# Two blocks' rows turned by VectorE and DMA moves instead of TensorE in a float32 decoder layer

## The chip, the cores and the metric

The kernel runs on one core of one Trainium2 chip. The metric is the device time of one execution in microseconds (us), the median of several runs. A profile of one execution gives the busy time of each engine: TensorE (PE, and PEld for its weight loads), VectorE (DVE), ScalarE (ACT), GpSimd (POOL), and SyncE (SP), which issues nearly all DMA transfers.

## The reference

One decoder layer over 2048 tokens of 1024 channels in float32: a normalised input goes through one combined projection into two mixers (a gated short convolution and a gated linear recurrence), their outputs through W_out back into x, then a multilayer perceptron (MLP) with a squared relu, then a last norm.

```python
    x = x + jnp.einsum('bsc,cd->bsd', y, w_out[l])
    h = rmsnorm(x, norm_mlp_g[l])
    z = jnp.square(jax.nn.relu(jnp.einsum('bsd,df->bsf', h, w_mlp_in[l])))
    x = x + jnp.einsum('bsf,fd->bsd', z, w_mlp_out[l])
```

The change concerns the second of these lines: the norm of x, with its weight, and the transposition of its rows that the third line needs.

## The kernel before

Tokens are worked in blocks of 512, two blocks (b and b+1) at a time, so the program goes through the same stages twice, for a first and a second pair. Every matrix product of two blocks is done with seven products instead of eight (a Strassen-Winograd scheme). The products are numbered 1 to 7 and run in the order 1, 2, 6, 5, 7, 3, 4 in the MLP (`ORDER`, L40). Each operand is split into a high and a low part of a shorter float format, `hi` by a copy on ScalarE and `lo` by a subtraction on VectorE (`split_into`, L196 to L198), and each product takes three matmuls (high by high, high by low, low by high).

Three stages matter here.

The out-projection (`pair_before_mlp`, L2135). Class `WOut` multiplies the mixers' outputs by W_out, product by product. A product has four tiles of 128 tokens with 18 matmuls each; after each tile VectorE adds the PSUM result into the residual `x` (`add`, L2112 to L2116). The products run in the order 1, 2, 6, 5, 3, 7, 4. The functions `in_sixth`, `in_fifth`, `in_third`, `in_seventh` and `in_fourth` are called after each tile of the product they are named for, and hold what the other engines do beside it. After product 3 block b's rows of x are complete; after product 4 block b+1's.

The norm and the turn. For each tile, ScalarE sums the squares (`square`, L2349), VectorE and ScalarE make the factor (`root`, L2360), and the scaled rows go to a tile `xs`: one half by VectorE, one by ScalarE (`scaled`, L2373, L2380 and L2381). The MLP needs the rows turned, with channels on partitions. Block b is turned in 32x32 blocks by VectorE (`cut_squares`, L2390) and then by DMA moves that bring every 32 partitions onto 128 (`move_squares`, L2400 to L2405); the norm weight is multiplied in after that (`gain_rows`, L2424). Block b+1 is turned by TensorE: `turn` (L1980) makes eight transposes of 128x128 into PSUM, and ScalarE copies each out, multiplying in the norm weight (L1991). Two of a pair's four turns stand inside product 4 of the out-projection and just behind it, two after the first and second MLP product (`turns`, L2478, called from `mlp`).

The MLP's first half (`mlp`, L2509, class `Up`, L605). Hidden columns come in eight groups of 512. The sequence starts with products 1 and 2 of groups 0, 1 and 2, which need block b alone, and goes on with their products 6, 5, 7, 3, 4, which need sums and differences of both blocks' turned rows (`rest`, L2482, `fifth`, L2496, `later_operands`, L2033). `Up.prepare` splits a weight tile two products ahead, `Up.sums` makes the weight sums, `Up.drain` (L671) takes results out of PSUM, applies the squared relu and spills to DRAM. The PSUM buffers are four of 2 x 512 columns. In the opening, three stay with product 1 of the three groups, and the fourth passes from one group's product 2 to the next.

What sets the order. Within the out-projection the order of TensorE, ScalarE and VectorE is that of the program text (`by_hand`, L2645). From the MLP on only TensorE's order is stated so; the order on ScalarE, VectorE and SP comes from the framework's list scheduler, by priority and by free buffers. SP is scheduled throughout. A DMA instruction on SP waits in order: what stands behind one that waits, waits too.

Of the kernel before, what the change touches and what calls it, by code (L numbers as in the profile page):

```python
# [9 lines left out]
F32 = mybir.dt.float32  # L10
# [38 lines left out]
T_ROOM = 15  # L49
LEADS = (0, 0, 2, 3, 2, 1, 2, 2, 2, 2, 2, 3, 2, 2)  # L50
# [41 lines left out]
def block_kernel(  # L92
# [11 lines left out]
    mlp_g_t,  # L104
# [12 lines left out]
    cp.tile([P, 120], F32, name="pad")  # L117
    hp = ctx.enter_context(tc.tile_pool(name="hp", bufs=2))
# [315 lines left out]
    def new_h():  # L434
        return (
            hp.tile([P, KD, TB], F32R, tag="h", name="h_hi"),
            hp.tile([P, KD, TB], F32R, tag="h", name="h_lo"),
        )
# [166 lines left out]
    class Up:  # L605
# [33 lines left out]

        def prepare(self, i):  # L640
            src = {1: "a11", 2: "a12", 6: "s2", 5: "a21", 7: "s3", 3: "a12", 4: "a22"}[i]
            self.ready[i] = split_new(getattr(self, src), wtile, "w")
# [27 lines left out]

        def drain(self, i, Z):  # L671
            def snap(ps):
                t = temp("snap")
                made_at["snap"] = nc.scalar.copy(t, ps).ins  # L674
                return t

            def square(t):
                if self.s < 3 or self.by_act:
                    nc.scalar.activation(t, t, AF.Relu)  # L679
                    nc.scalar.activation(t, t, AF.Square)  # L680
                else:
                    V.scalar_tensor_tensor(t, t, 0.0, t, MAX, MUL)
# [9 lines left out]
            elif i == 2:  # L692
                for j in range(2):
                    c = by_token(self.c11, j)
                    V.tensor_add(c, by_square(self.y, j), c)
                square(self.c11)
                keep(1, self.c11)
# [4 lines left out]
            elif i == 7:  # L702
                V.tensor_add(self.c22, self.x, self.c22)  # L703
                square(self.c22)
                keep(4, self.c22)
            elif i == 3:
                V.tensor_add(self.c12, self.w, self.c12)
                square(self.c12)
# [1271 lines left out]
    def turn(xs, t, r, g=None):  # L1980

        ps = psum("tps", (P, KD, P))
        for k in range(KD):
            nc.tensor.transpose(ps[:, k, :], xs[:, k // 4, k % 4 * P : (k % 4 + 1) * P], ident)
        sl = slice(t * P, (t + 1) * P)
        if g is None:
            for q in range(4):
                nc.scalar.copy(r[q][:, :, sl], ps[:, 2 * q : 2 * q + 2, :])
# [713 lines left out]
```

## Time and profile before

| | us |
|---|---|
| median of 3 runs | 2084.69 (2084.52 to 2084.88) |
| the profiled execution, its own time | 2084.75 |
| its span in the profile | 2082.9 |
| busy: PE, DVE, ACT, POOL | 2072.8, 1635.8, 1140.9, 46.4 |

The span is the time from the first to the last instruction; the execution's own time holds another 1.85 us around it. Rows of the instruction views begin with the start in us from the beginning of the span and the duration in us; "x4" behind a row is a count of merged instructions. "Matmul busy" is counted with the pipelined ends of matmuls, so the time between one start and the next is the better measure of what a matmul costs.

### The profile page before, as it was taken

What the parts mean: (1) busy time and instruction counts of PE and PEld (TensorE: products, weight loads), DVE (VectorE), ACT (ScalarE), POOL (GpSimd) and SP (SyncE); (2) the same over time, 40 slices, a digit from 0 to 9 for tenths busy, and PEclk for the clock granted to TensorE, in tenths of its full rate; (3) what the DMA queues carried; (4) which work ended last, traced back from release to release, by engine and by line L of the source; (5) the groups of instructions that cost most, each with busy time, mean ns of one, the idle gap of its engine ahead of it and who ended that gap; (6) DMA issues with size and microseconds to landing.
All of it is one profiled execution on the core that took longest, in us unless ns stands there. A gap on an engine that the chain in (4) does not pass through costs nothing.

```text
span 2082.9 us, 24925 instructions
## 1 busy us (share of the span) xinstructions
PE 2072.8 (100%) x9262; PEld 1707.4 (82%) x9262; DVE 1635.8 (79%) x1867; ACT 1140.9 (55%) x1485; POOL 46.4 (2%) x75
## 2 busy tenths in 40 slices
PE   9999999999999999999999999999999999999998
PEld 7888788888888888888888887888888888888886
DVE  6789898679766878999987776877885665887776
ACT  6789863376655544444555887234854333433344
POOL 0011000000000000000000100000000000000000
PEclk9999999999999999999999999999999999999999
DMA  9489688763787787777384557776343445944432
GB/s 341 166 296 330 242 324 348 269 222 120 262 317 281 265 296 301 271 282 281 121 313 164 210 182 249 266 272 222 132 182 122 175 149 212 353 150 143 142 122 81
DMA packets 201097, 477.76 MB, mean 229 GB/s; under 512 B 15248, under 2 KB 79760, under 8 KB 200976
## 3 DMA queue, kind: packets, MB, share of 16 engines
q1 hardware_dynamic: 199376, 471.45, 62.8%
q10 hardware_dynamic: 1568, 4.72, 0.6%
q8 instruction: 73, 1.20, 0.2%
q14 instruction: 48, 0.39, 0.1%
q0 software_dynamic: 32, 0.00, 0.0%
HBM read 313.58 MB, written 158.33 MB: 227 GB/s over the span
## 4 chain that ended last, share of the span: by engine, by line
PE 85%; DVE 5%; ACT 4%; issue 1%; DMA 1%; POOL 0%; SPq 0%; DVEq 0%; ACTq 0%; POOLq 0%
PE up L662 42%; PE dn L785 28%; PE wo_x L2103 6%; PE wo_w L2103 3%; PE wo_y L2103 2%; DVE xr L1303 1%; DVE v L1360 1%; PE ps_b L256 1%; ACT r L1324 1%; PE psri L1771 1%; ACT gi L1331 1%; DVE w_lo L1244 1%; PE ps_v L256 1%; PE ps_c L256 1%; PE dn L804 1%
## 5 line engine op out<-in xcount | busy, mean ns | idle before, releaser
L662 PE MATMUL up<-H,w_hi 128*128 128x512 f32 x2576 | 795.3, 390 | 0.0
L662 PEld LDWEIGHTS up<-H,w_hi 128*128 128x128 f32 x2576 | 482.3, 188 | 102.7 <-issue 1.8
L662 PE MATMUL up<-H,w_lo 128*128 128x512 f32 x1288 | 501.2, 389 | 0.0
L785 PE MATMUL dn<-w_hi,z_hi 128*128 128x512 f32 x864 | 336.1, 389 | 0.0
L785 PE MATMUL dn<-w_lo,z_hi 128*128 128x512 f32 x864 | 336.1, 389 | 0.0
L785 PE MATMUL dn<-w_hi,z_lo 128*128 128x512 f32 x864 | 336.1, 389 | 0.0
L662 PEld LDWEIGHTS up<-H,w_lo 128*128 128x128 f32 x1288 | 241.8, 188 | 50.4 <-DVE w_lo L198 0.2
L197 ACT CAST z_hi<-z 128x1024 fp32r<-128x1024 f32 x112 | 118.0, 1054 | 290.1 <-PE dn L785 250.6
L198 DVE TENSOR_TENSOR w_lo<-w,w_hi 128x1024 fp32r<-128x1024 f32 x156 | 190.2, 1221 | 70.6 <-ACT w_hi L197 25.8
L197 ACT CAST w_hi<-w 128x1024 fp32r<-128x1024 f32 x156 | 163.0, 1049 | 106.3 <-PE up L662 60.2
L785 PEld LDWEIGHTS dn<-w_lo,z_hi 128*128 128x128 f32 x864 | 162.2, 188 | 33.7
L785 PEld LDWEIGHTS dn<-w_hi,z_hi 128*128 128x128 f32 x864 | 162.2, 188 | 33.6
L785 PEld LDWEIGHTS dn<-w_hi,z_lo 128*128 128x128 f32 x864 | 162.2, 188 | 33.6
L817 DVE TENSOR_TENSOR x<-dn,x 128x1024 f32<-128x1024 f32 x108 | 131.1, 1220 | 22.5 <-PE dn L785 22.0
L198 DVE TENSOR_TENSOR z_lo<-z,z_hi 128x1024 fp32r<-128x1024 f32 x112 | 136.5, 1218 | 1.8 <-ACT z_hi L197 1.8
L2103 PE MATMUL wo_x<-w_o,y_hi 128*128 128x512 f32 x384 | 118.7, 390 | 0.0
L2103 PEld LDWEIGHTS wo_x<-w_o,y_hi 128*128 128x128 f32 x384 | 71.8, 188 | 14.8
L679 ACT ACTIVATE snap<-snap 128x1024 f32<-128x1024 f32 x36 | 38.3, 1063 | 82.4 <-DVE snap L703 32.5
L2103 PE MATMUL wo_x<-w_o,y_lo 128*128 128x512 f32 x192 | 74.9, 390 | 0.0
L2103 PE MATMUL wo_w<-w_o,y_hi 128*128 128x512 f32 x192 | 59.1, 389 | 0.0
L198 DVE TENSOR_TENSOR w_lo<-t,w_hi 128x1024 fp32r<-128x1024 f32 x32 | 39.1, 1222 | 19.7 <-PE dn L785 14.2
L674 ACT COPY snap<-up 128x1024 f32<-128x1024 f32 x32 | 32.4, 1014 | 36.1 <-PE up L662 35.6
(430 smaller groups left out, 3209.0 us busy)
## 6 DMA issues: line engine op xcount, KB each, us to landing
z<-d_z SPq DMA_DIRECT2D x112, 512.0 KB, 5.6
w_o<-d_sum SPq DMA_DIRECT2D x84, 512.0 KB, 6.9
w<-in_w_mlp_in_dram SPq DMA_DIRECT2D x64, 512.0 KB, 6.9
d_z<-snap SPq DMA_DIRECT2D x64, 512.0 KB, 3.1
d_sum<-sum_hi SPq DMA_DIRECT2D x49, 512.0 KB, 4.8
d_z<-z SPq DMA_DIRECT2D x48, 512.0 KB, 2.9
w<-in_w_mlp_out_dram SPq DMA_DIRECT2D x48, 512.0 KB, 8.3
raw<-in_w_in_dram SPq DMA_DIRECT2D x30, 512.0 KB, 6.9
```

The lines of the kernel that those rows point to most:

```text
L197: nc.scalar.copy(hi, src)
L198: return (lo_engine or V).tensor_tensor(lo, src, hi.bitcast(F32), SUB).ins
L256: nc.tensor.matmul(ps[:, j, :], ws[k // 4][:, k % 4, j * P : (j + 1) * P], hs(k), start=k == 0 and i == 0, stop=k == KD - 1 and i == len(p ...
L662: nc.tensor.matmul(ps[:, j, :], ws[:, k, j * P : (j + 1) * P], hs(k), start=i in (1, 2, 5) and k == 0 and n == 0, stop=k == 3 and n == len ...
L674: made_at["snap"] = nc.scalar.copy(t, ps).ins
L679: nc.scalar.activation(t, t, AF.Relu)
L785: nc.tensor.matmul(ps[t // 2][:, t % 2, :], zs[:, p, t * P : (t + 1) * P], ws[:, p, :], start=i in (1, 2, 5) and a == 0 and p == 0 and n == 0,
L804: nc.tensor.matmul(self.x[t // 2][:, t % 2, :], zs[:, p, t * P : (t + 1) * P], ws[:, p, :], start=False, stop=a == 1 and p == 1 and n == 2 ...
L817: V.tensor_add(xt[b, th, dh], ps[th], xt[b, th, dh])
L1244: tt(lo, r, hi.bitcast(F32), SUB)
L1303: stt(o, x_in[:, j, k : k + TB], par("rnn_conv_w", 8 * k + c), o, MUL, ADD)
L2103: nc.tensor.matmul(ps[t % 2][:, t // 2, :], ys[:, j, t * P : (t + 1) * P], ws[:, j, :], start=first and n == 1, stop=final and n == 6 * le ...
```

## The change

Both blocks are now turned in the same way, by VectorE's 32x32 transposes and DMA moves. `turn`, `turns` and `gain_rows` are gone, and TensorE transposes nothing. The norm weight comes in once as a row broadcast to all partitions (`full_g`, 512 KB, reordered on the host) and is multiplied in while the rows are scaled: both halves by VectorE with SCALAR_TENSOR_TENSOR, which reads x four elements apart. The moves are 16 of 128 KB per block instead of 8 of 256 KB for block b alone, with a raised priority. A tile's transposes stand one tile later than its scaling, ahead of the next tile's. The splits for product 7 stand beside product 5 instead of product 3. Since both blocks' tokens now stand in the same turned order, all results of the MLP's first half are put back into token order while they leave PSUM, in two halves. The order of ScalarE and VectorE is stated in the text on through the first ten MLP products (`open_mlp`); from the eleventh on it is the scheduler's again. The pool of two buffers for first operands becomes two pools of one.

```diff
-            V.tensor_scalar(to[1], of[1], rs, None, MUL)
-            nc.scalar.activation(to[0], of[0], AF.Copy, scale=rs)
+            for i in (1, 0):
+                g = full_g[:, i * 512 : i * 512 + 512].rearrange("p (g m) -> p g m", g=4)
+                to = xs[t][:, i, :].rearrange("p (g m) -> p g m", g=4)
+                of = x_half(b, t, i).rearrange("p (m g) -> p g m", g=4)
+                V.scalar_tensor_tensor(to, of, rs, g, MUL, MUL)
...
+        def cut_rows(t):
+            u = t // 2
+            for dh in (1, 0):
+                if (u, dh) not in pieces:
+                    pieces[u, dh] = temp("cut", (P, 4, 4, 2, 32))
+                V.transpose(
+                    pieces[u, dh][:, :, :, t % 2, :],
+                    xs[t][:, dh, :].rearrange("p (g k i) -> p g k i", k=4, g=4),
+                )
+
+        def move_rows(to, u):
+            if not to:
+                to.extend([temp("row", (P, 2, 2, 4, 64)) for _ in range(2)] for _ in range(2))
+            for dh in range(2):
+                for a in range(4):
+                    with tc.high_priority(SOONER):
+                        nc.sync.dma_start(
+                            to[dh][a // 2][:, a % 2, u].rearrange("p k x -> p (k x)"),
+                            pieces[u, dh][32 * a : 32 * a + 32].rearrange("p g k s i -> p (g k s i)"),
+                        )
...
+        def in_seventh(n, t):
...
+            if n == 3:
+                first_lo(1, 1)
+                square(b + 1, t, 1)
+                ups[0].hi(ORDER[0])
+                ups[0].lo(ORDER[0])
+                ups[0].hi(ORDER[1])
+
+        def in_fourth(n, t):
+            square(b + 1, t, 0)
+            if n == 0:
+                guard(b + 1)
+                ups[0].lo(ORDER[1])
+            else:
+                cut_rows(n - 1)
+            if n == 2:
+                move_rows(rows1, 0)
+            scaled(b + 1, t)
...
         product(4, X, False, in_fourth)
-        ups[1].prepare(ORDER[0])
-        return xs, raw0, r1, gm
+        ups[1].hi(ORDER[0])
+        cut_rows(3)
+        move_rows(rows1, 1)
+        ups[1].lo(ORDER[0])
+        return rows0, rows1
...
+        def rest(u):
+            if not t2:
+                t2.extend(temp("T2", (P, 2, 2, 4, 64)) for _ in range(2))
+            for ap in range(2):
+                t1 = r0[0][ap][:, :, u]
+                V.tensor_tensor(t1, r1[0][ap][:, :, u], t1, SUB)
+                V.tensor_tensor(t2[ap][:, :, u], r1[1][ap][:, :, u], t1, SUB)
...
+        at = [
+            lambda: (ups[0].load((1,)), ups[2].load((0,))),
+            lambda: (drain(0), rest(0), hi(3), lo(3)),
+            lambda: (added(1), hi(4), rest(1), lo(4), ups[0].sums(6), ups[1].load((1,)), squared(1)),
+            lambda: (drain(2), split_rows(6), hi(5), lo(5)),
+            lambda: (added(3), split_rows(5), squared(3), hi(6), lo(6)),
+            lambda: (drain(4), sub(r1[0], r1[1], r1[0]), ups[0].sums(3), hi(7), lo(7)),
+            lambda: (added(5), sub(t2, r0[1], t2), hi(8), split_rows(7), lo(8), squared(5)),
+            lambda: (drain(6), split_rows(3), hi(9), lo(9)),
+            lambda: (drain(7), hi(10), split_rows(4), lo(10)),
+            lambda: (added(8), ups[1].sums(6), hi(11), lo(11), ups[2].load((1,)), squared(8)),
+        ]
+        for n, fn in enumerate(at):
+            s, i = seq[n]
+            ups[s].multiply(i, H)
+            fn()
+        drain(OPEN - 1)
```

Here `hi` and `lo` are the two halves of `Up.prepare`, `added` the addition of a PSUM result to an earlier one, `squared` the squared relu and spill; the entry at place n stands behind the multiply of MLP product n, counted from 0.

339 lines of the change are left out of this document (152 added, 187 removed).

## The prediction

> **What bounds the kernel now.** I read the page's busy line first, then the chain of waits in order of time, then busy time by stage, then the instruction rows of the stage that the change rewrites.
>
> ```profile
> PE 2072.8 (100%) x9262; PEld 1707.4 (82%) x9262; DVE 1635.8 (79%) x1867; ACT 1140.9 (55%) x1485; POOL 46.4 (2%) x75
> ...
> 414.61 28.56 PE wo_x L2103 x126
> 443.17 0.87 PE tps L1984 x8
> 444.04 4.10 PE wo_x L2103 x18
> 448.14 0.87 PE tps L1984 x8
> 449.02 5.46 PE up L662 x24
> 454.48 0.87 PE tps L1984 x8
> 455.35 5.46 PE up L662 x24
> 460.81 0.87 PE tps L1984 x8
> 461.68 266.67 PE up L662 x1176
> ```
>
> Each piece of the chain starts where the one before it ended: through this stage TensorE never waits, so a matmul taken out there is worth its whole duration, and a wait put in costs its whole length. 28.56 us for 126 matmuls is 0.2267 each: a tile of 18 takes 4.08, a product of the out-projection (72) 16.32, a product of the MLP (1176 matmuls in 266.67, so 24) 5.44. The four pieces "tps" are the turns that the change removes. The other engines have little room in places:
>
> ```profile
> core 0: us, PE busy (x) PEld busy (x) DVE busy (x) ACT busy (x) POOL busy (x), PEclk, DMA share, GB/s
> 381.97:398.29 16.32, 16.32 (x73) 13.51 (x73) 6.40 (x7) 2.40 (x6) 0.00 (x0) 1.00 0.63 227
> 398.29:414.61 16.32, 16.32 (x73) 13.51 (x73) 12.31 (x27) 7.69 (x14) 0.00 (x0) 1.00 0.64 236
> 414.61:430.93 16.32, 16.32 (x73) 13.51 (x73) 12.68 (x19) 8.14 (x14) 0.00 (x0) 1.00 0.97 307
> 430.93:449.02 18.09, 18.09 (x89) 15.16 (x89) 15.06 (x30) 11.38 (x23) 0.00 (x0) 1.00 0.50 180
> 460.90:482.00 21.10, 21.10 (x99) 17.58 (x97) 20.44 (x34) 16.74 (x32) 0.00 (x0) 1.00 0.25 84
> 482.00:515.00 33.00, 33.00 (x147) 27.34 (x146) 30.95 (x34) 22.98 (x24) 0.00 (x0) 1.00 0.27 94
> ```
>
> The rows are products 5, 3, 7 and 4 of the first pair, then MLP. VectorE is busy 15.06 of 18.09 us in product 4 and 51.4 of 54.1 from 460.90 to 515. The granted clock is 1.00 throughout.
>
> **Part 1, the turns go.** The program has eight turns of eight transposes: four stand in the chain above (0.87 each), four at the same places of the second pair.
>
> ```profile
> L1984 PE MATMUL tps<-ident,xs x64: 270/272/273, 443.0 to 1476.2; 128*128 128x128 f32 x64
> 450.16 4.22 ACT L1991 ACTIVATE r<-tps,gm 128x128 f32<-128x128 f32 x16
> ```
>
> 8 x 0.87 = 7.0 us leave TensorE, all on the path. ScalarE loses the copies out of PSUM (16 in 4.22 us; 32 per pair), which lay beside matmuls: no direct gain.
>
> **Part 2, VectorE's step per tile of 128 rows.** In products 3 and 4 a tile now costs VectorE the add, two block transposes (of the tile before), four small instructions for the factor, and two SCALAR_TENSOR_TENSOR with the norm weight, each reading x four elements apart. For block b+1 the transposes and the strided reads are new.
>
> ```profile
> 410.57 1.31 DVE L2395 STREAM_TRANSPOSE cut<-xs 128x512 f32<-128x512 f32 x2
> 411.81 0.71 DVE L2116 SCALAR_TENSOR_TENSOR x<-wo_w,rB,x 128x512 f32<-128x512 f32 x1
> 412.44 1.21 DVE L198 TENSOR_TENSOR y_lo<-u,y_hi 128x1024 fp32r<-128x1024 f32 x1
> 413.57 0.15 DVE L2366 SCALAR_TENSOR_TENSOR rs_a<-ss,ss 128x1 f32<-128x1 f32 x1
> ...
> 414.29 0.68 DVE L2380 TENSOR_SCALAR xs<-x,rs_x 128x512 f32<-128x512 f32 x1
> 438.82 0.49 DVE L2380 TENSOR_SCALAR xs<-x,rs_x 128x512 f32<-128x512 f32 x1
> 405.44 1.21 ACT L2381 ACTIVATE xs<-x,rs_x 128x512 f32<-128x512 f32 x1 [0.68 <-DVE rs_x L2370]
> 438.82 0.73 ACT L2381 ACTIVATE xs<-x,rs_x 128x512 f32<-128x512 f32 x1 [0.68 <-DVE rs_x L2370]
> 433.90 2.49 DVE L2434 TENSOR_TENSOR H<-raw,H 128x512 fp32r<-128x512 f32 x4
> 439.45 1.04 ACT L197 CAST w_hi<-w 128x1024 fp32r<-128x1024 f32 x1
> ```
>
> From start to start: two transposes 1.24, an add 0.63, a 1024-wide SUB 1.13, the factor 0.72, a 512-wide SUB 0.62. The new multiply is not in the trace. Its floor is the add's 0.63 (same kind, contiguous). Its ceiling adds what ScalarE pays for these strided reads (1.21 against 0.73): 1.11. I take VectorE's own surcharge, 0.68 against 0.49: 0.82. A step is then 0.63 + 1.24 + 0.72 + 1.64 = 4.23 us against 4.08 of matmuls (3.85 at the floor, 4.81 at the ceiling). Product 3 had such a step already: its SUB of 1.13 moves to product 5, where VectorE is busy 6.40 of 16.32.
>
> [...]
>
> **Part 3, the turned rows of block b+1 arrive by DMA.** Before, they came through PSUM; now each block has 16 moves of 128 KB on SP (block b had 8 of 256 KB, block b+1 none), the last eight only after the last tile's transposes. Behind them on SP stand spills of x and MLP weight loads. The nearest rows are block b's moves, 1 MB in four:
>
> ```profile
> 411.92 3.97 SPq L2402 DMA_DIRECT2D raw<-cut  x4
> ...
> 420.75 2.81 SPq L2402 DMA_DIRECT2D raw<-cut  x4
> ...
> L2402 SPq DMA_DIRECT2D raw<-cut x1: 1532/1532/1532, 414.3 to 414.3; - x1
> ...
> DMA to landing us min/median/max: 5.5/5.5/5.5
> ...
> L2402 SPq DMA_DIRECT2D raw<-cut x2: 608/635/662, 422.2 to 422.9; - x2
> ...
> DMA to landing us min/median/max: 8.5/8.5/8.6
> ...
> L622 SPq DMA_DIRECT2D w<-in_w_mlp_in_dram x1: 373/373/373, 425.0 to 425.0; - x1
> ...
> DMA to landing us min/median/max: 10.3/10.3/10.3
> ```
>
> First issue to last landing: 7.9 us where the DMA engines were free (411.92 to 414.3 + 5.5) and 10.7 where they were full (420.75 to 422.9 + 8.5). I take the middle, 9.3.
>
> Now the chain of the first pair. The stated order puts the split of the first MLP weight ahead of product 4's first add. That weight lands at 425.0 + 10.3 = 435.3; CAST and SUB (1.04 + 1.13) end at 437.5, though the first tile is ready at 435.0. First tile: add, next weight's SUB, guard (0.2), factor, multiplies: 4.3, to 441.8. Three steps of 4.23: 454.5. Last transposes: 455.7. Moves land at 465.0. Meanwhile VectorE does a SUB (1.13), the differences of the first half (4 x 0.62), a SUB and the PSUM addition for the second product (2 x 0.62), until 461.7; then it waits for the moves. This is the change's new wait: the second half's four differences, the last of which starts at 465.0 and ends at 465.7. Queued behind it on VectorE: a weight SUB, three weight sums (3.4), four SUBs of operand 6 (2.5), a SUB, and the PSUM addition of the fourth product (1.2), 9.4 in all, to 475.1. The sixth MLP product needs the PSUM buffer that this addition frees, and its start without a wait is 447.25 + 5 x 5.44 = 474.45. Late by 0.6 us, in each pair: **1.2 us** given back.
>
> With 7.9 for the moves VectorE's own work ends at 473.6 and nothing is lost; with 10.7 it is 2.0 per pair. With the multiply at its floor nothing is lost.
>
> **Part 4, the rest.** After that, the stated ten products ask VectorE for 20 SUBs or sums of 1024 (1.13) and 36 halves (0.62), 44.9 us in 54.4: it regains its lead by the ninth. The norm weight's 512 KB (before, 4 KB on POOL) load while the DMA share is 0.63 (product 5), 16 us ahead of use; were they late, only product 3's scaling would move, whose rows are wanted a product later. PSUM copies in two halves instead of one cost ScalarE (55% busy) about 0.1 us each, an estimate. All this costs nothing while TensorE has two products prepared; without that cover a weight's CAST and SUB, 2.2 us, lie open (rival C).
>
> **Sum.** On the profiled execution, 2084.75 us (2082.9 of span and 1.85 around it): -7.0 + 1.2 = 2078.95. That execution stands 0.06 above the median: **2078.9**.
>
> **Rivals.**
> A. The strided multiply costs what ScalarE pays (1.11). For it: the same access pattern; against it: VectorE's smaller surcharge. The last transposes end at 458.05, the third MLP product's weight SUB at 459.2, 0.6 after its third matmul would want it (458.6); the rows land at 467.35, and the sixth product waits 2.3 more. 2.9 per pair: -7.0 + 5.9, 2083.6.
>
> B. The moves wait in the queue, and the kernel gets slower. The spills of x and four MLP weight loads went out just where the last moves now belong:
>
> ```profile
> 442.44 9.06 SPq L584 DMA_DIRECT2D d_x<-x  x4
> 451.59 3.28 SPq L622 DMA_DIRECT2D w<-in_w_mlp_in_dram  x4
> ```
>
> Two of those spills and the four loads are 3 MB, out by 451.59 + 3.28 = 454.9; with 7 us to land, an estimate between the landings quoted above (5.5 and 8.5), they are through near 461.6. If they stay ahead, the rows land at about 461.6 + 7.9 = 469.5: the fifth product waits 1.9 for its weight SUB, the sixth 3.2 more. 5.1 per pair: 2087.9; with A's multiply as well, about 2094. It decides from a landing after 467.9, 12.2 us after the first issue, where 3.5 us per pair eat the gain. For it: the row above; against it: DMA stood idle before 451, and the moves are given priority.
>
> C. The stated order ends after ten products, where VectorE was 94% busy (30.95 of 33.00). If one weight's CAST and SUB lies open there per pair, 2 x 2.2: 2082.1. Against it: the ten products leave slack.
>
> **How the numbers follow.** Forecast with its own range 2077.7 to 2080.5: 0.50. A 0.18, B 0.23, C 0.09. A difference of 0.2%, 4.2 us, is about what a measurement of this kernel can tell from no change, so faster means below 2080.5 and slower above 2088.9. Faster: the forecast and 0.03 of A (its milder half), 0.53. Same: the rest of A (0.15), C, and 0.03 of B, 0.27. Slower: the rest of B, 0.20. Nothing offers more than 7.0 us, so the range begins just under 2077.7, at 2077.2, and ends at 2089 in B's milder half.
>
> **What would show it.** No "tps" piece in the chain; product 4 and the MLP adjoining. Right: a TensorE gap under 1 us before the sixth MLP product, released by VectorE's addition; the multiplies near 0.85 us; last rows landing 8 to 10.5 us after the first issue. Wrong: gaps before the third or fifth MLP product, moves issued behind weight loads, a multiply above 1.1, or gaps from the eleventh product on.

## The result and the profile after

The changed kernel takes 2095.18 us (median of 6 runs, 2092.87 to 2099.37) against 2084.78 (6 runs, 2084.41 to 2085.04): a ratio of 1.0051, 95% interval 1.0038 to 1.0064. It is slower by 10.4 us, where 2078.9 was forecast. The profiled execution took 2092.87, 2.3 us below the median; its span is 2091.1. The rows below account for that execution; where the slower ones lose their 2.3 us and more, no trace shows.

The busy line of its page, and then TensorE's rows in order of time that carry a wait (start, duration, in brackets the idle time before it and what ended it):

```profile
PE 2072.3 (99%) x9198; PEld 1701.8 (81%) x9198; DVE 1659.4 (79%) x1899; ACT 1110.5 (53%) x1441; POOL 45.7 (2%) x74
```

```profile
443.17 0.73 PE L2100 MATMUL wo_x<-w_o,y_hi 128*128 128x512 f32 x2 [0.28 <-DVE x L2113]
...
470.93 0.73 PE L676 MATMUL up<-H,w_hi 128*128 128x512 f32 x2 [1.41 <-ACT w_hi L645]
472.19 0.50 PE L676 MATMUL up<-H,w_lo 128*128 128x512 f32 x1 [0.53 <-DVE w_lo L649]
480.68 0.70 PE L676 MATMUL up<-H,w_hi 128*128 128x512 f32 x2 [1.60 <-DVE snap L688]
...
679.18 0.50 PE L676 MATMUL up<-H,w_lo 128*128 128x512 f32 x1 [1.47 <-DVE w_lo L200]
...
734.55 0.47 PE L427 MATMUL bc<-diag_hi,ones_r 128*128 128x512 f32 x1 [1.08 <-DVE diag_hi L409]
...
1492.11 0.73 PE L676 MATMUL up<-H,w_hi 128*128 128x512 f32 x2 [1.55 <-ACT w_hi L645]
1493.37 0.80 PE L676 MATMUL up<-H,w_lo 128*128 128x512 f32 x1 [0.53 <-DVE w_lo L649]
...
1501.86 0.70 PE L676 MATMUL up<-H,w_hi 128*128 128x512 f32 x2 [1.62 <-DVE snap L688]
```

TensorE, which had no wait between 290 and 2064 us before, now stands still ahead of and inside the fifth MLP product (1.94 us), ahead of the sixth (1.60), and nearly the same again in the second pair. The fifth waits for a weight's cast and SUB, the sixth for VectorE's addition out of PSUM. In the first pair it also waits 0.28 us ahead of product 4's last tile for VectorE's add into x. Busy time by stage adds something that no row shows as a wait:

```profile
core 0: us, PE busy (x) PEld busy (x) DVE busy (x) ACT busy (x) POOL busy (x), PEclk, DMA share, GB/s
...
460.00:470.00 10.00, 9.53 (x42) 7.51 (x41) 6.35 (x10) 0.16 (x1) 0.00 (x0) 1.00 0.89 279
470.00:475.00 5.00, 3.54 (x10) 2.53 (x11) 4.02 (x4) 4.97 (x8) 0.00 (x0) 0.77 0.30 103
475.00:480.00 5.00, 4.08 (x16) 2.96 (x14) 5.00 (x8) 4.00 (x7) 0.00 (x0) 0.88 0.69 222
```

The mean granted clock of the two five-microsecond stretches is 0.77 and 0.88. The first MLP product starts at 447.38, so the sixth should start at 447.38 + 5 x 5.44 = 474.58; it starts at 480.68, 6.1 late. 3.54 of that are the three waits. 1.6 lie in the nine matmuls from 472.53 to 476.17, which take 3.64 us where they would take 2.04 at 0.2267 each: the slower clock, 0.53 in that stretch. The other 1.0 lies in steps of 0.1 to 0.3 us between starts, most of them beside the waits, that no row counts as waiting. In the second pair the sixth product is 6.2 late. From the sixth product to the end of the MLP's first half (480.68 to 763.05, against 477.86 to 756.45 before) the first pair loses 3.8 more: 1.47 and 1.08 of waits, and 1.2 in such small steps, most of them beside these two waits. So, against the profiled execution of before: -7.0 for the turns, +12.3 for the two openings, +3.8 for that stretch, -1.1 for a shorter tail, and +0.1 for what is left (0.7 around the wait in product 4, less 0.4 gained ahead of it, and roundings): 2084.75 + 8.1 = 2092.85, measured 2092.87.

Why the fifth and sixth wait is read from three queues. SP's, with the landing of its eight moves, then ScalarE's, then VectorE's rows in order of time:

```profile
457.04 5.13 SPq L2392 DMA_DIRECT2D row<-cut  x8
462.27 2.51 SPq L624 DMA_DIRECT2D w<-in_w_mlp_in_dram  x4
...
L2392 SPq DMA_DIRECT2D row<-cut x8: 555/606/614, 457.0 to 461.6; - x8
...
DMA to landing us min/median/max: 2.5/2.6/2.8
```

```profile
469.84 1.04 ACT L645 CAST w_hi<-w 128x1024 fp32r<-128x1024 f32 x1 [13.52 <-DMA w<-in_w_mlp_in_dram]
```

```profile
440.29 2.17 DVE L2371 SCALAR_TENSOR_TENSOR xs<-x,rs_x,gain 128x512 f32<-128x512 f32 x2
442.36 0.75 DVE L2113 SCALAR_TENSOR_TENSOR x<-wo_x,rB,x 128x512 f32<-128x512 f32 x1
...
447.01 0.74 DVE L2113 SCALAR_TENSOR_TENSOR x<-wo_x,rB,x 128x512 f32<-128x512 f32 x1
...
456.31 1.29 DVE L2381 STREAM_TRANSPOSE cut<-xs 128x512 f32<-128x512 f32 x2
...
464.42 0.69 DVE L2514 TENSOR_TENSOR row<-row 128x512 f32<-128x512 f32 x1 [0.71 <-DMA row<-cut]
...
466.48 0.69 DVE L2515 TENSOR_TENSOR T<-row 128x512 f32<-128x512 f32 x1
470.91 1.23 DVE L649 TENSOR_TENSOR w_lo<-w,w_hi 128x1024 fp32r<-128x1024 f32 x1 [3.75 <-ACT w_hi L645]
472.06 1.22 DVE L635 TENSOR_TENSOR s<-w,w 128x1024 f32<-128x1024 f32 x1
...
475.71 2.49 DVE L200 TENSOR_TENSOR H<-T,H 128x512 fp32r<-128x512 f32 x4
478.12 1.22 DVE L649 TENSOR_TENSOR w_lo<-w,w_hi 128x1024 fp32r<-128x1024 f32 x1
479.25 1.28 DVE L688 TENSOR_TENSOR snap<-up,snap 128x512 f32<-128x512 f32 x2
```

The four MLP weight loads, which went out at 451.59 before, now go out at 462.27, behind the last eight moves; SP's queue waits 1.7 us ahead of these moves (455.25 to 457.04) for VectorE's transposes, and the loads stand behind that wait too. Their weight is cast at 469.84; ScalarE had waited 13.5 us for it, VectorE 3.75. Behind this SUB, in the written-out order, stand three weight sums, operand 6, another SUB, and only then the addition (479.25) that the sixth product needs. The rows themselves landed in time: VectorE waited 0.71 us for them. All four differences of the second half stand behind that landing, from 464.42 to 467.17: the wait of the first ends only when the last of the eight moves is in (issued at 461.6, landed 2.8 later).

### The profile page after: what moved, and what is told of

The parts are those of the page before. It is cut to its first block, busy times and chain, and to the rows that moved or that the text cites. A ratio compares the mean times of both kernels' runs of the same rounds, so it can differ in the third digit from the quotient of the medians.

```text
span 2091.1 us, 24901 instructions
## 1 busy us (share of the span) xinstructions
PE 2072.3 (99%) x9198; PEld 1701.8 (81%) x9198; DVE 1659.4 (79%) x1899; ACT 1110.5 (53%) x1441; POOL 45.7 (2%) x74
## 4 chain that ended last, share of the span: by engine, by line
PE 63%; DVE 1%; DMA 0%; issue 0%; ACT 0%; ACTq 0%
PE up L676 28%; PE dn L804 28%; PE wo_x L2100 3%; PE wo_w L2100 2%; PE wo_y L2100 1%; PE psri L1790 1%; PE dn L823 1%; DVE x L860 0%; DMA w<-in_w_mlp_in_dram 0%; DMA w_o<-d_sum 0%; DVE H L200 0%; PE sps L2054 0%; DVE rs_q L860 0%; DVE u L2234 0%; PE bc L427 0%
## 5 line engine op out<-in xcount | busy, mean ns | idle before, releaser
L200 DVE TENSOR_TENSOR w_lo<-w,w_hi 128x1024 fp32r<-128x1024 f32 x134 | 163.0, 1220 | 61.1 <-PE dn L804 24.4
L199 ACT CAST w_hi<-w 128x1024 fp32r<-128x1024 f32 x134 | 139.4, 1048 | 100.8 <-PE up L676 63.0
L688 DVE TENSOR_TENSOR snap<-up,snap 128x512 f32<-128x512 f32 x96 | 62.3, 684 | 79.6 <-PE up L676 70.1
```

Source lines behind the costliest of these rows:

```text
L199: nc.scalar.copy(hi, src)
L200: return (lo_engine or V).tensor_tensor(lo, src, hi.bitcast(F32), SUB).ins
L688: V.tensor_add(by_token(c, j), by_square(ps, j), by_token(c, j))
```

## The experiments

All times are medians; each ratio is against the kernel before on the same chip, with its 95% interval. The kernel before had medians of 2084.61 to 2084.86 there, so differences between runs of different groups hold some tenths of a us of the chip.

**1 to 4: the multiply, SP's order, both, and the written-out order.** The first moves the four weight loads ahead of the last moves:

```diff
-        move_rows(rows1, 1)
+        ups[0].load((1,))
+        ups[2].load((0,))
+        with tc.issue_after(made_at["w1"]):
+            move_rows(rows1, 1)
...
-            lambda: (ups[0].load((1,)), ups[2].load((0,))),
+            lambda: None,
```

> Only the order on SP's queue is changed: the four weight loads for the MLP products after the second are issued ahead of the last eight moves of turned rows, in both pairs. Theory T (the strided multiply lengthens VectorE's chain by 1.6 us, and the weights then queue behind the late moves; each alone opens gaps of TensorE, and the clock dips after them): the weights land near 465 us of the first pair instead of 470, the 1.4 us gap released by ScalarE's cast of that weight goes, but the moves land near 469 instead of 464, so the gaps move to the differences of the second half and 1 to 3 us of the 6.1 per pair come back at most: 2089 to 2094. Rival R1 (the multiply's stride alone): no change, 2095. Rival R2 (the order on SP alone): the gaps before the fifth and sixth MLP product vanish in both pairs, 12.3 us come back, 2083.

The second makes the multiply contiguous and moves the channel order into the weight loads:

```diff
-                "(h k p) (f c) -> f h p k c", p=P, h=2, f=2
+                "(h g k i) (f c) -> f h i g k c", i=32, g=4, h=2, f=2
...
-                g = full_g[:, i * 512 : i * 512 + 512].rearrange("p (g m) -> p g m", g=4)
-                to = xs[t][:, i, :].rearrange("p (g m) -> p g m", g=4)
-                of = x_half(b, t, i).rearrange("p (m g) -> p g m", g=4)
-                V.scalar_tensor_tensor(to, of, rs, g, MUL, MUL)
+                g = full_g[:, i * 512 : i * 512 + 512]
+                V.scalar_tensor_tensor(xs[t][:, i, :], x_half(b, t, i), rs, g, MUL, MUL)
```

> The scaled multiply reads x and writes its result contiguously; the channel order that the stride produced is moved into the access pattern of the first MLP weight's loads (32 partitions and groups of four exchanged). Queue order as in the changed kernel. T: the multiply falls from 1.04 to about 0.63 us start to start and VectorE's step from 4.64 to 3.85, the last transposes end near 454.4 instead of 457.5, the rows land near 461 to 463 and the weights near 467; no gap before the fifth MLP product, 2.5 to 2.9 us per pair left before the sixth, some of the clock dip with it: 2086 to 2089. R1: all gaps of the opening vanish, about 2083. R2: the weights still wait behind the moves, and nothing changes by more than 1 us: 2094 to 2095.

The third has both edits.

> Both edits together: contiguous multiply and weight loads ahead of the last moves. T: no gap of TensorE before the fifth and sixth MLP products in either pair, granted clock 1.00 from 440 to 500 us; what is left of the loss is the 3.9 us of gaps and clock after the tenth MLP product of the first pair: 2079 to 2083, faster than the kernel before by 0.1 to 0.3%. R1 and R2: the same as with their own edit alone, 2083; if neither cause is the real one, 2090 or more.

The fourth ends the written-out order with the out-projection:

```diff
-        open_mlp(ups, seq, r0, r1, Z)
         stack.close()
         stack.enter_context(tc.manual_schedule(engines={nc.tensor.engine}))
+        open_mlp(ups, seq, r0, r1, Z)
```

> The written-out order of ScalarE and VectorE ends with the out-projection; the ten MLP products are left to the planner's own order. SP's order is as in the changed kernel. T: the weight still lands near 470 us and the multiply still costs 1.04, so the gaps before the fifth and sixth product stay within 2 us of 6 per pair; the gaps near 679 and 734 us of the first pair may go or not: 2090 to 2098. Rival R3 (the stated order itself holds work back that could run): the gaps of the opening go, 2083 or below.

Measured: 2095.73 (1.0054, 1.0037 to 1.0070), 2091.57 (1.0032, 1.0020 to 1.0043), 2090.93 (1.0032, 1.0021 to 1.0044), 2099.26 (1.0073, 1.0057 to 1.0088). T missed all of them: the first came out at R1's number, the second 2.6 above T's range, the third at the "2090 or more" that its expectation kept for the case that neither cause is the real one, the fourth 1.3 above T's range. The first run's VectorE row of the late differences and its TensorE rows:

```profile
467.85 0.69 DVE L2517 TENSOR_TENSOR row<-row 128x512 f32<-128x512 f32 x1 [4.77 <-DMA row<-cut]
```

```profile
471.78 0.50 PE L676 MATMUL up<-H,w_lo 128*128 128x512 f32 x1 [2.45 <-DVE w_lo L649]
480.27 1.09 PE L676 MATMUL up<-H,w_hi 128*128 128x512 f32 x2 [3.20 <-DVE snap L688]
```

With the loads first the rows are late instead: the first late difference starts at 467.85, 3.4 us later, and the waits have only changed their owner. The third run's rows show what is left when the multiply is short too:

```profile
465.11 0.69 DVE L2515 TENSOR_TENSOR row<-row 128x512 f32<-128x512 f32 x1 [6.03 <-DMA row<-cut]
...
476.10 1.28 DVE L688 TENSOR_TENSOR snap<-up,snap 128x512 f32<-128x512 f32 x2
```

```profile
477.53 0.70 PE L676 MATMUL up<-H,w_hi 128*128 128x512 f32 x2 [3.21 <-DVE snap L688]
```

VectorE idles 6 us for the rows and then has 12.3 us of work up to the end of the one addition that is wanted. The weight SUB and the three sums in it (4.8 us) needed no rows: they could have been done while it idled. The second pair of the third run still waits in the fifth product too (2.32, for such a SUB). The chain behind whatever lands last, not the landing alone, became the suspect (T2 below). The stated order is not worse than the planner's: without it the kernel is 4 us slower. The short multiply is worth 3.6 us in the changed kernel and 4.8 with the loads first.

**5 to 8: the order behind the landing.** The fifth run changes the changed kernel's written-out order alone and moves the addition ahead of the sums and of operand 6:

```diff
-            lambda: (added(1), hi(4), rest(1), lo(4), ups[0].sums(6), ups[1].load((1,)), squared(1)),
-            lambda: (drain(2), split_rows(6), hi(5), lo(5)),
-            lambda: (added(3), split_rows(5), squared(3), hi(6), lo(6)),
+            lambda: (added(1), hi(4), rest(1), lo(4), ups[1].load((1,)), squared(1)),
+            lambda: (drain(2), hi(5), lo(5)),
+            lambda: (added(3), ups[0].sums(6), split_rows(6), squared(3), hi(6), lo(6), split_rows(5)),
```

> The changed kernel with one edit of VectorE's and ScalarE's written-out order: the PSUM addition after the fourth MLP product, which frees the buffer for the sixth, goes ahead of the three weight sums and the SUBs of operand 6 (6.2 us of VectorE that only the seventh product needs). Theory T2 (that addition stands at the end of a chain of some 9.4 us behind whatever lands last, and the written-out order put 6.2 us of it there): the weights still land near 470 us, the gap of 1.9 us before and in the fifth product stays, the gap of 1.6 us before the sixth goes, in both pairs, and some of the clock's dip with it: 2089 to 2092. Rival R4 (the rows and weights land too late, whatever the order behind them): the sixth product's gap stays or moves to the seventh, 2094 to 2096.

The sixth has the loads first and the weight work ahead of the late rows:

```diff
+            lambda: (added(1), hi(4), lo(4), ups[0].sums(6), ups[1].load((1,)), squared(1)),
+            lambda: (drain(2), hi(5), lo(5), rest(1)),
+            lambda: (added(3), split_rows(6), squared(3), hi(6), lo(6), split_rows(5)),
```

> The strided multiply is kept. Weight loads are issued ahead of the last eight moves (as in the first experiment), and VectorE's written-out order takes what depends on the weights first: the fifth product's weight SUB, the three sums, the sixth's weight SUB, then the differences of the late rows, the PSUM addition after the fourth product, operand 6, the seventh product's weight, operand 5. T2: VectorE does 6 us of weight work while the rows are still under way; rows land near 468, differences end at 470.5, the addition at 472 against a need at 474.5; no gap before the fifth and sixth products in either pair, granted clock 1.00 there: 2095.2 - 12.3, so 2081 to 2084. R4: rows at 468 hold the sixth product as they did in the first experiment, 2092 to 2096. R1 (the multiply's stride must go first): 2090 or more.

The seventh adds to the sixth the handover (from the eleventh product on, the half additions after products 7 and 3 wait until the next product's weight SUB is issued), the eighth the contiguous multiply as well. The handover:

```diff
+                los[m] = made_at["split"]
...
-                ups[s].drain(i, Z)
+                with tc.issue_after(los[n + 1]) if n + 1 in los and i in (7, 3) else nullcontext():
+                    ups[s].drain(i, Z)
```

> As the run before, and from the eleventh product on VectorE's two half additions after the fifth and sixth product of a group of seven (those numbered 7 and 3) are held behind the weight SUB of the next product, where the planner had put one half ahead of it. Theory of the handover: the gap of 1.47 us near 679 us of the first pair and the dip after it go, 1.5 to 3 us less than the run before, 2079 to 2082. Rival (the planner only moves the wait to another product): no change within 1 us, or slower.

> As the run before, with the contiguous multiply (the channel order moved into the first MLP weight's loads). T2: the opening was gapless already, so nothing but noise changes, within 1 us of the run before. R1 (the stride decides): 3 us or more faster than the run before.

Measured: 2097.83 (1.0064, 1.0050 to 1.0077), 2089.91 (1.0024, 1.0015 to 1.0033), 2087.31 (1.0010, 1.0001 to 1.0019), 2083.78 (0.9995, 0.9986 to 1.0004). The fifth run is a miss: the sixth product's wait went, as expected, but the seventh's weight SUB was then late by 0.94 and the eighth's addition by 2.92 (first pair). With weights landing near 470, moving the addition forward only moved the wait. The sixth run gained 5.3 us, not the 12.3 expected; 1.05 and 2.27 us stay ahead of the sixth product of the two pairs, 1.74 and 0.15 ahead of the eighth. The seventh confirms the handover, 2.6 us; this is what it undid, VectorE's rows of the changed kernel:

```profile
677.30 0.69 DVE L688 TENSOR_TENSOR snap<-up,snap 128x512 f32<-128x512 f32 x1 [4.15 <-PE up L676]
677.91 2.35 DVE L200 TENSOR_TENSOR w_lo<-w,w_hi 128x1024 fp32r<-128x1024 f32 x2
```

The planner had put half an addition, which waits 4.15 us for TensorE, ahead of the SUB that TensorE needs next (679.18 above). The eighth run's 3.5 us for the short multiply went against T2 (within 1 us) and for R1 (3 or more).

**9 and 10: additions ahead of all else.** The ninth changes the eighth's kernel, the tenth is the same with the strided multiply:

```diff
+            lambda: (drain(2), hi(5), lo(5)),
+            lambda: (added(3), rest(1), split_rows(6), squared(3), hi(6), lo(6), split_rows(5)),
+            lambda: (drain(4), hi(7), lo(7)),
+            lambda: (added(5), sub(r1[0], r1[1], r1[0]), ups[0].sums(3), hi(8), split_rows(7), lo(8), sub(t2, r0[1], t2), squared(5)),
```

> As the run with the contiguous multiply, the early weight loads and the handover edit, with one more move in VectorE's written-out order: the PSUM additions after the fourth and the sixth product go ahead of everything that later products need (the first ahead of the differences of the late rows, the second, with the weight SUB of the eighth product, ahead of the differences for operand 7 and the fourth sum). In the run before, TensorE still stood 0.68 us ahead of the sixth and 1.74 us ahead of the eighth product of each pair, released by these two additions, 4.9 us in all. Theory T2: both gaps go in both pairs, nothing else changes, 2083.8 - 4.9, so 2078 to 2080, faster than the kernel before by 0.2 to 0.3%. Rival R4 (the rows land too late whatever the order): the gaps move to the seventh and ninth product, which now wait for operand 6 and operand 7, 2083 to 2086.

> The same with the strided multiply of the changed kernel kept: only SP's order, VectorE's written-out order and the handover differ from the changed kernel. T2: the rows land 2 to 3 us later than with the contiguous multiply, and the written-out order has 3 us of weight work to put in their place; the operand of the seventh product is the next at risk: 0 to 3 us above the run with the contiguous multiply, 2079 to 2083. R1 (the stride decides): 5 us or more above it.

Measured: 2085.29 (1.0003, 0.9995 to 1.0012) and 2088.65 (1.0020, 1.0011 to 1.0029). Another miss for T2, and R4's picture: in the ninth run the waits sit at the seventh (0.53) and ninth product (1.16) of each pair instead, and beyond the tenth. The tenth lies 3.4 us above the ninth, between T2's 0 to 3 and R1's 5 or more.

**11 and 12: another queue.** The last eight moves go out on POOL's queue, in the changed kernel and in the eighth run's:

```diff
-        move_rows(rows1, 1)
+        move_rows(rows1, 1, nc.gpsimd)
```

> The changed kernel with one edit: the last eight moves of turned rows of each pair are issued on POOL's queue (otherwise empty there) instead of SP's, so neither they nor the four weight loads wait behind each other in a queue. Theory Q (SP's one queue is what delays: eight moves take it 5.1 us to issue, and the loads stand behind them): the weights land near 463 us instead of 470, the rows no later than 465; the gaps of 1.9 us before and in the fifth product go in both pairs, the sixth product's gap is left: 2088 to 2091. Theory D (the DMA engines themselves are full from 457 to 470 us, the moves at some 200 GB/s against 370 to 410 of the weight loads, so whatever the queue the same bytes land by the same time): the weights come earlier and the rows later, rows near 468 to 470, and the sixth product's gap grows by what the fifth's loses: 2093 to 2097.

> The fastest kernel so far (contiguous multiply, loads early, weight work ahead of the late rows, handover) with the last eight moves on POOL's queue. Q: rows land near 461 instead of 465, the sixth product's gap of 0.7 us goes in both pairs; the eighth's 1.74 us, which stands behind VectorE's later work, gets smaller: 2080 to 2083. D: rows land at 465 or later, no gain within 1 us: 2083 to 2085.

Measured: 2094.90 (1.0051, 1.0036 to 1.0066) and 2092.34 (1.0035, 1.0023 to 1.0048). In the eleventh run theory D holds, number and picture. The twelfth is a miss for both theories: it is 8.6 us slower than the eighth, where D allowed 1. Its weight is cast 1.9 us later than the eighth's (465.23 against 463.31), VectorE idles 6.56 us for it instead of 3.56, and TensorE waits 2.11 and 3.10 us ahead of the two sixth products, with a granted clock of 0.75 and 0.50 in the five microseconds around and behind them. That is D's direction, with a price that D had not seen. In the eleventh run the weight comes 2.8 us earlier than in the changed kernel and the rows 3.3 us later; ScalarE's cast and VectorE's first late difference:

```profile
467.03 1.06 ACT L645 CAST w_hi<-w 128x1024 fp32r<-128x1024 f32 x1 [11.14 <-DMA w<-in_w_mlp_in_dram]
```

```profile
467.69 0.69 DVE L2514 TENSOR_TENSOR row<-row 128x512 f32<-128x512 f32 x1 [4.42 <-DMA row<-cut]
```

Moves ahead of loads, loads ahead of moves, and both at once, with the changed kernel's written-out order: 2095.2, 2095.7, 2094.9. What the moves ask of the DMA engines is seen in the same stretch of the kernel before and of the changed one, then in the changed one also while moves run alone (458 to 463) and while the loads run, and in the eleventh run while both do:

```profile
447.00:470.00 23.00, 23.00 (x116) 19.30 (x115) 17.12 (x39) 20.26 (x53) 0.00 (x0) 1.00 0.46 160
```

```profile
458.00:463.00 5.00, 5.00 (x22) 3.86 (x21) 4.93 (x7) 0.00 (x0) 0.00 (x0) 1.00 0.73 195
...
463.00:469.00 6.00, 6.00 (x28) 4.96 (x27) 3.38 (x6) 0.00 (x0) 0.00 (x0) 1.00 0.96 314
447.00:470.00 23.00, 22.53 (x99) 18.06 (x97) 19.10 (x33) 5.05 (x11) 0.00 (x0) 1.00 0.74 228
```

```profile
455.00:467.00 12.00, 12.00 (x54) 9.67 (x53) 8.21 (x11) 0.89 (x1) 4.49 (x8) 1.00 0.98 329
```

The DMA share of the stretch rises from 0.46 to 0.74. One after the other, moves hold the queue at a share of 0.73, then the loads fill the engines (0.96); both at once fill them for twelve microseconds (0.98). In this written-out order, the queue decides who is late, not whether someone is. D's "full from 457 to 470" is too much for the changed kernel, where the share is 0.86 in that stretch, and its 370 to 410 GB/s are rates of later stretches that mix loads and spills (375 from 570 to 580, 409 from 620 to 630); these loads moved 314 from 463 to 469.

**13 to 17: fewer bytes ahead, and an order for the new arrivals.** The thirteenth run puts the last two spills of x behind the moves, in the eighth's kernel:

```diff
-            keep_half(b, t)
+            if t < 3 or b % 2 == 0:
+                keep_half(b, t)
...
+        with tc.issue_after(made_at["move"]):
+            keep_half(b + 1, 3)
```

> The run with contiguous multiply, early loads, weight work first and handover (2083.8 us), with one edit: the last two spills of x of the pair's second block (1 MB) are issued behind the last moves instead of ahead of the weight loads. Theory D (from 447 to 468 us the DMA engines are full, so what lands is set by the bytes ahead of it): 1 MB at some 400 GB/s is 2.5 us, weights and rows land 2 to 2.5 us earlier, VectorE idles less there, the sixth product's gap of 0.68 us goes in both pairs and the eighth's of 1.74 shrinks by what VectorE is ahead: 2080 to 2082.5. Theory V (VectorE's own work in the ten products is what is too much, wherever it waits): the gaps only move, 2083 to 2085.

The fourteenth changes the ninth's kernel (`squared(5)` moves one entry down, behind the copy in `drain(6)`), the fifteenth has both edits:

```diff
-            lambda: (added(5), sub(r1[0], r1[1], r1[0]), ups[0].sums(3), hi(8), split_rows(7), lo(8), sub(t2, r0[1], t2), squared(5)),
-            lambda: (drain(6), split_rows(3), hi(9), lo(9)),
+            lambda: (added(5), sub(r1[0], r1[1], r1[0]), ups[0].sums(3), hi(8), split_rows(7), lo(8), sub(t2, r0[1], t2)),
+            lambda: (drain(6), squared(5), split_rows(3), hi(9), lo(9)),
```

> The run in which both additions go ahead of what later products need (2085.3 us), with one edit of ScalarE's written-out order: the relu and square after the sixth product's addition (2.1 us) go behind the copy that frees the PSUM buffer for the ninth product, where they stood ahead of it. V with the order as its only lever: the ninth product's gap of 1.16 us goes in both pairs, the gaps of 0.8 to 0.95 us near 521 and 549 us, after the written-out order ends, stay or shrink: 2082 to 2084. Rival: those later gaps grow by what the ninth's loses, 2085.

> Both edits of the two runs before together. D and the order together: no gap in the ten products of either pair, less than 1 us of gaps up to 560 us: 2079 to 2081.5, faster than the kernel before by 0.15 to 0.3%. V: 2083 to 2085.

Measured: 2083.67 (0.9995, 0.9986 to 1.0004), 2085.68 (1.0003, 0.9994 to 1.0012), 2085.99 (1.0006, 0.9997 to 1.0015). None gained: the thirteenth has V's number, the fourteenth its rival's (the ninth product then waits 0.70 for a weight SUB instead of 1.16 for the copy), the fifteenth lies above both theories. Yet the thirteenth's weight was cast at 460.99 instead of the eighth's 463.31, as D expected. (That the engines are full from 447 to 468 was D's estimate; in the seventeenth run the share from 447 to 470 is 0.78.) VectorE did not use it; its row and ScalarE's in the thirteenth run:

```profile
470.57 1.23 DVE L649 TENSOR_TENSOR w_lo<-w,w_hi 128x1024 fp32r<-128x1024 f32 x1 [3.61 <-ACT w_hi L645]
```

```profile
469.49 1.05 ACT L645 CAST w_hi<-w 128x1024 fp32r<-128x1024 f32 x1 [4.14 <-PE up L676]
```

The sixth product's weight SUB waits for a cast that waits until TensorE frees a tile, and the late differences, whose rows had come, stand behind it. In the fifteenth run the same wait is 3.12. So the next edit, on the fifteenth's kernel:

```diff
-            lambda: (drain(2), hi(5), lo(5)),
-            lambda: (added(3), rest(1), split_rows(6), squared(3), hi(6), lo(6), split_rows(5)),
+            lambda: (drain(2), rest(1), hi(5), lo(5)),
+            lambda: (added(3), split_rows(6), hi(6), lo(6), squared(3), split_rows(5)),
```

> As the run with all edits before it (2086.0 us), with two places of the written-out order changed: the differences of the late rows go ahead of the sixth product's weight SUB (whose cast waits for TensorE's slot until 469.3, while the rows have landed near 467), and ScalarE casts the seventh product's weight ahead of the square after the fourth. Theory T4 (since the late spills let rows and weights land by 461 and 467, VectorE's idle of 3.6 us ahead of that weight SUB is what is left, an order that no longer fits the arrivals): VectorE does the differences in that idle time, operand 6 is done near 475 instead of 478, the gaps in the ten products (0.53 and 0.68 us per pair) go, those of 0.9 us near 521 us shrink: 2080 to 2083. Theory V (the work of VectorE and ScalarE in the ten products is too much in any order): 2083 to 2086.

> The same with the strided multiply of the changed kernel. The rows land some 3 us later, near 470, so the sixth product's weight SUB waits behind them. T4: 1 to 4 us above the run with the contiguous multiply. V: the same within 1 us.

Measured: 2081.94 (0.9989, 0.9980 to 0.9998) and 2082.39 (0.9988, 0.9979 to 0.9997): both faster than the kernel before by 0.1%, with intervals that end just below 1, and 12.8 us faster than the changed kernel in the second case, with its strided multiply untouched. T4 holds for the order; on the multiply V's number was right. VectorE's stretch that was idle, in the seventeenth run, and the waits of TensorE that it has left in the first pair:

```profile
460.00:470.00 10.00, 10.00 (x45) 8.26 (x44) 9.85 (x13) 4.84 (x6) 0.00 (x0) 1.00 0.95 307
470.00:475.00 5.00, 5.00 (x24) 4.13 (x23) 4.97 (x8) 2.80 (x6) 0.00 (x0) 1.00 0.84 275
475.00:480.00 5.00, 5.00 (x24) 4.14 (x23) 3.74 (x6) 4.97 (x8) 0.00 (x0) 1.00 0.26 109
```

```profile
519.61 0.73 PE L676 MATMUL up<-H,w_hi 128*128 128x512 f32 x2 [0.87 <-ACT snap L704]
...
547.60 0.72 PE L676 MATMUL up<-H,w_hi 128*128 128x512 f32 x2 [0.49 <-ACT snap L704]
```

From 460 to 470 VectorE works 9.85 of 10 us, where the changed kernel had 6.35, and TensorE does not wait in the ten products. What waits remain, 2.8 us in the whole execution, come after them but for 0.27 in the second out-projection; without them its 2082.7 (the profiled execution) would be 2079.9, an estimate.

## Why the prediction was wrong, point by point

- **The turns (part 1): right.** No turn is left in TensorE's rows. In the second pair, product 7 of the out-projection to the first MLP product takes 32.66 us (1435.79 to 1468.45) instead of 34.33 (1429.23 to 1463.56): two turns of 0.87, within 0.1. In the first pair the same stretch is only 1.0 shorter, because of the wait in product 4.
- **The multiply (part 2): a term sized too small.** Two take 2.07 from start to start (440.29 to 442.36), 1.04 each, against 0.82; a step of VectorE is then 4.65 (442.36 to 447.01), not 4.23. Its price by VectorE's own surcharge was the wrong neighbour; ScalarE's (1.11) was nearer. The longer step already costs TensorE 0.28 of wait in product 4 (443.17), which no part of the prediction had.
- **The chain to the rows (part 3): right up to their landing, by luck in part.** Forecast and measured: first add 437.5, 437.7; last transposes end 455.7, 457.6 (the multiply's 0.42 in each of four steps, and 0.2 of the start); last rows land 465.0, 464.4 (VectorE's first late difference, released by them after 0.71 of wait). From first issue to landing that is 7.3 us, below the 9.3 taken and its lower bound of 7.9, since each move landed 2.5 to 2.8 us after its issue where the quoted neighbours took 5.5 to 8.5. The 7.9 was not the time of free engines either: the DMA share in its stretch (411.92 to 419.8) was 0.79, against 0.97 in that of the 10.7. The two errors cancel.
- **The step that failed** is the next sentence of part 3, "Queued behind it on VectorE: a weight SUB, three weight sums ...", 9.4 in all, to 475.1. The length is right (470.91 to the end of the addition at 480.5 is 9.6). But the SUB's weight was taken to be there. Part 3 noted that spills and weight loads stand behind the moves on SP, and nothing priced that those loads come late: they landed near 469.8, and the chain began 5.2 us late (470.91 against 465.7). A smaller error lies under it: part 3 put one of the four late differences behind the landing, and all four came behind it, to 467.17. With the weight there, the 9.6 us behind them would have ended near 476.8, an estimate: 2.2 late instead of the 0.6 forecast.
- **What hid it (part 4): the cover was gone.** "All this costs nothing while TensorE has two products prepared" left out that the fifth product's weight is one of the loads in question, so that nothing was prepared for it. The PSUM copies in two halves cost ScalarE 1.07 us for two (17.2 us of busy time for 32) against 1.01 for a whole one (16.2 for 16): 0.06 more, where part 4 put 0.1.
- **Rival B had the size by luck, and the wrong sign of the queue.** It priced moves behind loads at 5.1 us per pair, with A 2094 (its 454.9 + 7 is 461.9, not 461.6, which hardly matters). The loads were behind the moves, and that cost 6.1, clock included. Experiment 1 made B's own case: 2095.7. Its condition, a landing after 467.9, was not needed. "DMA stood idle before 451" holds from 449 on (a share of 0.04 from 449 to 451.6); from 442 the share is 0.28.
- **Rival A:** the short multiply gains 3.6 us in the changed kernel's order, 4.8 with the loads first, 3.5 and 3.4 in two later orders, but 0.45, within the runs' spread, in the last. Its price seems to depend on how full VectorE's order is behind it, which was argued from these pairs and not varied by itself.
- **Rival C came on top, in part:** after the tenth product there are 2.55 us of waits in the first pair and none in the second, for its 2.2 in each. Only the 1.47 of them wait for a weight's SUB; the handover edit, made for that one, brought 2.6 back. (C's 2082.1 leaves out part 3's 1.2; with it the sum is 2083.3.)
- **Not in the sum at all:** the clock. The prediction took a wait to cost its whole length and no more; the slower matmuls behind the waits cost 1.6 us of the first opening's 6.1, and 1.7 of the second's 6.2 (nine matmuls from 1493.37 to 1497.10, at a granted clock of 0.55).

Shown is that neither SP's order or queue alone (2095.7, 2094.9) nor the addition's place alone (2097.8) brings anything back, that loads first and a new order together do (2089.9), that with the same transfers the written-out order alone is worth 4 us (2085.99 to 2081.94), and that with an order fitted to the arrivals the strided multiply is nearly free. Not shown is how much of that last step is due to each of its two moved places, whether the late spills are needed in the last order, and whether the later waits near 520 and 548 us go with an order written on to the fourteenth product; none of these was tried.

## What to carry to other kernels

When work moves from an engine to DMA, price the transfers that it pushes back as well as the ones that it adds: follow every load that shares the queue and the engines to the first instruction that wants it (here four loads went out at 462.27 instead of 451.59, and TensorE waited 1.94 us for their weight's cast and SUB). Where an engine's order is written out, put what can run during a landing ahead of what waits for it, and look after each edit whether that order still fits the arrivals, since a wait that is removed can show up one or two products later until the idle time itself is filled (0.94 and 2.92 us in the fifth run, 0.53 and 1.16 in the ninth). Judge a dearer instruction by the idle time beside it, not by its duration: the same multiply cost between 0.45 and 4.8 us here, by the order around it.

## What the runs showed of the hardware that was not expected

**The clock after short stops.** After some stops of TensorE the granted clock fell to about half (0.53 over 3.64 us from 472.53 in the changed kernel, 0.57 over 4 us in the sixth run), and after others it stayed at 1.00. The second pair of the sixth run (a stop of 2.27 us that ends at 1496.85) and the first pair of the first run (2.45 ending at 471.78, then 3.20 ending at 480.27):

```profile
1493.00:1497.00 4.00, 1.73 (x9) 1.15 (x8) 3.93 (x7) 2.08 (x4) 0.00 (x0) 1.00 0.34 136
1497.00:1501.00 4.00, 4.00 (x11) 3.17 (x12) 2.90 (x5) 3.97 (x6) 0.00 (x0) 0.57 0.24 98
1501.00:1505.00 4.00, 4.00 (x19) 3.30 (x18) 4.00 (x7) 3.28 (x6) 0.00 (x0) 1.00 0.10 39
```

```profile
473.00:477.00 4.00, 4.00 (x18) 3.01 (x17) 3.96 (x5) 2.33 (x5) 0.00 (x0) 1.00 0.03 9
477.00:481.00 4.00, 0.80 (x3) 0.67 (x3) 4.00 (x7) 0.84 (x1) 0.00 (x0) 0.92 0.00 0
481.00:485.00 4.00, 4.00 (x13) 3.12 (x13) 3.26 (x5) 3.17 (x5) 0.00 (x0) 0.65 0.34 135
```

2.27 was followed by a clock of 0.57 (11 matmuls in 4 us instead of 18), 2.45 by none of it, 3.20 by 0.65. In the changed kernel 1.41 and 0.53 close together were enough (0.53 over the nine matmuls behind them), and 1.60 ending at 480.68 was not (1.00 from 480 to 485). In the sixth run the nine matmuls behind the stop take 3.68 us (1496.85 to 1500.53) instead of 2.04, so the stop of 2.27 costs some 3.9 in all, and the length alone does not decide. What does decide, no run here shows.

**The price of an issue.** SP issues a 128 KB move in 0.64 us (eight in 5.13) and a 512 KB weight load in 0.63 (four in 2.51). SP's queue therefore fed these moves at 128 KB per 0.64 us, 205 GB/s, and the DMA engines moved 195 then (458 to 463), at a share of 0.73, against 314 at 0.96 while the loads ran (463 to 469): while these moves held the queue, they left the engines short.
